# Fewer head tiles among the index scores, eight bisection rounds at once, masks behind the values' tiles

## The chip, the core and the metric

The kernel runs on one core of a Trainium2 chip. The time is that of one execution on the device, in microseconds. Three executions of the kernel before took 1706.53, 1705.96 and 1699.86 us; the median is 1705.96. The core's engines are named as the profile names them: PE multiplies matrices (PEld loads its weights), DVE, ACT and POOL work element by element, SP issues most of the DMAs.

## What is computed

One step of a streaming encoder layer on 1024 prompt rows and 64 sample rows of width 1024, all in float32. The normalised input is projected to the heads' queries, keys and values of two attention branches, to index queries, index keys and index weights, and to gates. Branch a attends only to the 256 keys with the best index score of each query (a quarter of the keys for the sample rows); branch b to a band of chunks with a bias. Both are projected, gated, summed and projected again, and an MLP follows. The part that the change touches:

```python
s = relu(einsum('bqhd,bsd->bqhs', q_idx, k_idx))       # 8 index heads of 64
score = einsum('bqh,bqhs->bqs', w_idx, s)              # one score per query and key
score = where(key_chunk <= query_chunk, score, -inf)
_, idx = top_k(score, 256)                             # per query
logits = einsum('bqhd,bqkhd->bhqk', q, k[idx]) * HEAD_DIM ** -0.5
p = softmax(logits);  out = einsum('bhqk,bqkhd->bqhd', p, v[idx])
```

The outputs include the new keys and values of both branches.

## The kernel before

Each float32 factor is split into a high and a low part (`split`), and a product is three matmuls, on lines 156, 157 and 158 (`three`), or two where one factor's parts are stacked (`two`, lines 164 and 165). The input stays in SBUF transposed (`xnT`). Rows are handled in nine tiles: eight of 128 prompt rows and one of 64 sample rows.

*Keys, queries, scores.* `stage_keys(i)` projects index keys and weights of row tile i (264 columns a matmul), `stage_queries(i)` the index queries (320 columns), both into the two `acc` banks of PSUM. Readers of a keys bank are among others `kd` (L311), `aw` (L319) and `sg` (L320). `norms(i)` makes the norm factors, and `stage_scores(i)` turns the keys into columns (`index_keys`, the transposes of L232) and, for row tiles 2 to 7 and the sample tile, multiplies the turned queries with all keys seen so far: for each of eight heads one or two `s` banks of up to 512 columns (four banks in rotation), which ACT rectifies and scales (L381) and DVE adds to the row tile's scores `work` (L383 for the first head, L385 for the others). Row tiles 0 and 1 need no selection, they see at most 256 keys.

*Head tiles.* `project_heads` is a generator: for vb, kb, qb, ka, va and qa in this order it loads and splits 512 columns of weights and multiplies each of the nine row tiles by them, 24 matmuls of 512 columns for a full row tile, then evacuates the result (values by L527; keys and queries by a square L530, a sum L531, a norm factor, L535), turns it (L485) and parts it into high and low (ACT L124, DVE L148 or L491). Each `next` makes one such head tile. The instructions of these last operations are kept in order in the list `parted`, which holds one entry for every tile turned or, of the values, only for branch a. A head tile's accumulator comes from the iterator `turn`: the first `FIRST` tiles use the `acc` banks, later ones by turns `acc` and `wide`, `wide`. While the scores run, the other four banks are the `s` banks; behind the scores these become four `wide` banks. `stage_scores(i, between)` calls `next` behind the heads that the dictionary names, and what is left runs behind the scores (`for _ in heads`).

*Selection.* `choose` finds the 256th best score of each row by bisection on the bits of a float: counts of positive scores (L617), signs (L627 to L636), then 31 rounds. In a round `cand` sets one more bit (L640), DVE counts three row tiles (L617) and ACT three (L622) against it, and L647 and L648 keep the bit or not. `mask_out(j)` then makes the mask of one of the six row tiles on DVE (L666 to L673, the scan of L669 among them) and POOL (L674).

*Gates.* `gate` projects 128 gate columns on all rows, in chunks of 384, 384 and 320, and L686 scales the result by row. Behind the fourth gate attention begins.

*What sets the order.* The order on each engine is made when the program is built: a scheduler places each recorded instruction as its inputs and buffers allow, and `tc.issue_after(x)` keeps instructions from being placed ahead of instruction x. Round `30 - b` is bound in this way to `parted[(30 - b) * 38 // 31]`, so that the rounds spread over the head tiles, and the masks to the last weight split of the gates.

Of the kernel before, what the change touches and what calls it, by code (L numbers as in the profile page):

```python
# [24 lines left out]
NT = TP // P  # L25
# [5 lines left out]
DFF = 4096  # L31
EPS = 1e-6
RING = 5
FIRST = 8
WARM = 18
BIG = 1e30
HIDDEN = -2.0e38
# [7 lines left out]
def kernel(  # L45
# [80 lines left out]
    last = {}  # L126
# [212 lines left out]
    def stage_queries(i):  # L339
        if i < 2:  # L340
            return
        rows = P if i < NT else TS
        qd = state[i][-3]
        z0, _ = project(i, acc(), parts["queries"], SPLIT)
        copy(qd[:rows, 0:5, 0, :], z0[:rows, :320].rearrange("p (h d) -> p h d", d=HD))
        apply_rope(qd[:rows, :, 0, :], i, rows, H)
        nc.gpsimd.tensor_copy(qd[:rows, :, 1, :], qd[:rows, :, 0, :])
# [84 lines left out]
    def norms(i):  # L432
        stage_norms(i)
        if i + 2 <= NT:
            xts[i + 2] = load_x(i + 2)
# [4 lines left out]
    cut_piece(2, x2)  # L440
    stage_keys(4)
    stage_keys(5)
    with tc.issue_after(last["projected"].ins):
        norms(2)
        norms(3)
        x4 = take_piece(4)
        for nm, g in (("qa", qnorm_a), ("ka", knorm_a), ("kb", knorm_b)):
            load(gains[nm], bcast(g, HD))
        for half in (slice(0, HD), slice(HD, P)):
            load(gain_qb[half], bass.AP(tensor=qnorm_b.tensor, offset=qnorm_b.offset, ap=[[1, HD], [1, 1]]))  # L450
        nc.gpsimd.tensor_scalar(gain_qb, gain_qb, HD ** -0.5, 1.0, op0=ALU.mult, op1=ALU.mult)
        for i in range(3):
            stage_scores(i)
    stage_queries(4)
    stage_queries(5)
    cut_piece(3, x3)
    with tc.issue_after(last["projected"].ins):
        norms(4)
# [102 lines left out]


    heads = project_heads()
    stage_scores(NT - 3, {7: heads})
    stage_scores(NT - 2, {3: heads, 7: heads})
    stage_scores(NT - 1, {3: heads, 7: heads})
    stage_scores(NT, {3: heads, 7: heads})
    close_pool("ix")

    masks = open_pool("masks")  # L570
# [34 lines left out]
    def choose(vector, scalar):  # L605
# [30 lines left out]
            nc.vector.tensor_scalar(w, w, col(sgn, j), None, op0=ALU.mult)  # L636
        nc.vector.memset(bits, 0)
        for b in range(30, -1, -1):
            with tc.issue_after(parted[(30 - b) * 38 // 31]):
                nc.vector.tensor_scalar(cand, bits, 1 << b, None, op0=ALU.bitwise_or)  # L640
            for j, w in enumerate(ws):
                against = col(cand.bitcast(F32), j)
                if j < nv:
                    count(j, w, against, ALU.is_lt)
                else:
                    balance(j, w, against)
            nc.vector.tensor_tensor(ok, cnt, lim, op=ALU.is_le)  # L647
            nc.vector.copy_predicated(bits, ok, cand)  # L648
# [67 lines left out]
    with tc.issue_after(state["last"].ins):  # L716
        for _ in range(TOPK_S // 8):
            m8 = tk.tile([TS, 8], F32, tag="m8", name="m8", bufs=2)
            nc.vector.max(out=m8, in_=work_s)
            nc.vector.match_replace(out=work_s, in_to_replace=m8, in_values=work_s, imm_value=TAKEN)  # L720
        nc.vector.tensor_scalar(mask_s, work_s, 0.5 * (HIDDEN + TAKEN), -BIG, op0=ALU.is_gt, op1=ALU.mult)
        mask_out = choose([2, 3, 4], [5, 6, 7])
    nc.sync.dma_start(mask_below[TS:], mask_s)
    todo = [(mix, h) for mix in "ba" for h in range(H)]
    first_head = load_head(*todo[0], kv)
# [8 lines left out]
    for g in range(0, EARLY, 4):  # L734
        ws = []
        for k in range(KB):
# [3 lines left out]
            lo = pj.tile([P, 512], F32R, tag="wlo", name="wlo", bufs=11)  # L740
            split(raw, hi, lo, lo_on_vector=True)
            ws.append((hi, lo))
        lows = last["lo"]
        for q in range(4):
            gate(g + q, [(h[:, q * P:(q + 1) * P], l[:, q * P:(q + 1) * P]) for h, l in ws])
            while behind and q == 2:
# [2 lines left out]
            if g + q == EARLY - 2:  # L749

                with tc.issue_after(last["turned"].ins):
                    nc.scalar.activation(warm, eps, AF.Exp)

        with tc.issue_after(lows.ins):
            for j in range(6):
                mask_out(j)
    for nm in ("tk", "pj", "works", "fw"):
        close_pool(nm)

# [728 lines left out]
```

## Time and profile before

| | |
|---|---|
| median of three executions | 1705.96 us |
| the profiled execution, its own time | 1701.1 us |
| its span, first to last instruction | 1699.3 us |
| mean granted clock of PE | 0.996 |
| PE, DVE, ACT, POOL busy | 1678.4, 1169.3, 934.4, 393.1 us |
| head tiles behind the scores begin | 163.06 us |
| first bisection round, first mask, attention | 186.4, 411.6, 460.8 us |

The profile is of one execution, and all its times are microseconds from the span's start. Matmuls are pipelined in it: the time of one matmul is longer than the distance to the next one's start, and it is that distance which counts for PE. A bracket behind a row, such as `[2.39 <-POOL kd L333]`, is the idle time of the engine ahead of that instruction, and the instruction that ended it.

### The profile page before, as it was taken

Reading aid. Unit: us, or ns where it says so; the run is one execution under the profiler, and the core shown is the slowest. Engines: PE = TensorE matmul, PEld = TensorE weight load, DVE = VectorE, ACT = ScalarE, POOL = GpSimd, SP = SyncE. Lnnn points to the kernel's source line nnn. Section 1 sums busy time; section 2 is a strip of 40 time slices with the busy share of each in tenths; the row PEclk is TensorE's granted clock in tenths of the full one; section 3 lists DMA queues with packets and bytes.
Section 4 is the critical chain, followed back from the end, with each engine's and each line's share of the span. In section 5 each row is a group of like instructions: output and inputs, shape, how many; then the busy total and the mean of one; then the engine's idle time right before and its main releaser. Section 6 shows DMA issues by size and latency. Waiting matters only on the chain.

```text
span 1699.3 us, 30465 instructions
## 1 busy us (share of the span) xinstructions
PE 1678.4 (99%) x10501; PEld 1543.6 (91%) x10501; DVE 1169.3 (69%) x2748; ACT 934.4 (55%) x1876; POOL 393.1 (23%) x524
## 2 busy tenths in 40 slices
PE   9999999999889999999999999999999999999999
PEld 8987888889889999999999999999999988888887
DVE  7855898879757788874454347666687649656794
ACT  8765688784256777774443347544454346343431
POOL 4434313506243343432343440000000000000000
PEclk9999999999989999999999999999999999999999
DMA  8135366663388877645544459555566599765652
GB/s 277 37 118 155 112 170 169 185 218 94 109 196 194 205 177 174 162 113 162 167 146 145 174 168 311 172 186 182 178 209 196 196 293 300 231 205 174 199 188 90
DMA packets 281195, 303.11 MB, mean 178 GB/s; under 512 B 40209, under 2 KB 202513, under 8 KB 281041
## 3 DMA queue, kind: packets, MB, share of 16 engines
q1 hardware_dynamic: 251920, 265.63, 54.0%
q10 hardware_dynamic: 29120, 35.53, 6.0%
q8 instruction: 83, 1.36, 0.3%
q14 instruction: 72, 0.58, 0.1%
HBM read 207.98 MB, written 93.08 MB: 177 GB/s over the span
## 4 chain that ended last, share of the span: by engine, by line
PE 70%; DMA 5%; DVE 3%; ACT 2%; issue 1%; POOL 1%; SPq 0%; ACTq 0%; DVEq 0%
PE x L156 6%; PE x L157 6%; PE x L158 6%; PE acc L156 6%; PE acc L158 6%; PE acc L157 6%; PE pt L814 3%; PE pg L156 2%; PE pe L156 2%; PE pg L158 2%; PE pe L158 2%; PE pe L157 2%; PE pg L157 2%; PE po L830 2%; PE s L164 2%; PE po L829 2%
## 5 line engine op out<-in xcount | busy, mean ns | idle before, releaser
L124 ACT ACTIVATE hi<-hw 128x1024 fp32r<-128x1024 f32 (+1 forms) x108 | 99.9, 932 | 159.2 <-PE x L158 56.3
L157 PE MATMUL x<-lo,hi 128*128 128x512 f32 (+1 forms) x440 | 169.5, 385 | 0.0
L158 PE MATMUL x<-hi,lo 128*128 128x512 f32 (+1 forms) x440 | 169.1, 385 | 0.0
L156 PE MATMUL x<-hi 128*128 128x512 f32 (+1 forms) x440 | 165.1, 385 | 0.0
L148 DVE TENSOR_TENSOR lo<-hw,hi 128x1024 fp32r<-128x1024 f32 (+1 forms) x108 | 113.8, 1061 | 47.9 <-ACT hi L124 46.5
L150 POOL TENSOR_TENSOR lo<-raw,hi 128x512 fp32r<-128x512 f32 x74 | 98.4, 1339 | 130.1 <-ACT hi L124 115.6
L124 ACT ACTIVATE hi<-raw 128x512 fp32r<-128x512 f32 x104 | 64.3, 626 | 96.3 <-PE acc L157 20.8
L622 ACT ACTIVATE nth<-work,cand 128x768 bf16<-128x768 f32 (+2 forms) x93 | 96.6, 1039 | 13.5 <-DVE cand L640 9.5
L826 DVE TENSOR_TENSOR pl<-pt,ph 128x512 fp32r<-128x512 f32 (+2 forms) x152 | 90.9, 615 | 16.7 <-ACT ph L124 16.3
L157 PEld LDWEIGHTS x<-lo,hi 128*128 128x128 f32 x440 | 82.7, 188 | 16.6
L156 PEld LDWEIGHTS x<-hi 128*128 128x128 f32 x440 | 82.7, 188 | 16.6
L158 PEld LDWEIGHTS x<-hi,lo 128*128 128x128 f32 x440 | 82.7, 188 | 16.5
L156 PE MATMUL acc<-xnT,hi 128*128 128x384 f32 (+1 forms) x288 | 97.2, 337 | 0.0
L157 PE MATMUL acc<-xnT,hi 128*128 128x384 f32 (+1 forms) x288 | 95.1, 330 | 0.0
L158 PE MATMUL acc<-xnT,lo 128*128 128x384 f32 (+1 forms) x288 | 94.9, 330 | 0.0
L157 PE MATMUL wide<-wlo,xnT 128*128 128x512 f32 x240 | 94.2, 394 | 0.0
L158 PE MATMUL wide<-whi,xnT 128*128 128x512 f32 x240 | 93.7, 391 | 0.0
L156 PE MATMUL wide<-whi,xnT 128*128 128x512 f32 x240 | 92.2, 394 | 1.3 <-DVE work_s L385 1.3
L124 ACT ACTIVATE ph<-pt 128x512 fp32r<-128x512 f32 (+3 forms) x168 | 80.1, 514 | 23.3 <-PE pt L814 18.6
L801 POOL TENSOR_SCALAR mw<-mw,sm 128x640 f32<-128x640 f32 (+1 forms) x64 | 56.7, 885 | 127.6 <-DVE sm L800 123.4
L164 PE MATMUL s<-kh,qT 128*128 128x384 f32 (+4 forms) x208 | 77.1, 372 | 3.5 <-DMA kh<-kT_b 1.9
L830 PE MATMUL po<-pl,vhl 128*128 128x256 f32 (+1 forms) x304 | 79.5, 293 | 0.4 <-DVE pl L826 0.3
(693 smaller groups left out, 5731.9 us busy)
## 6 DMA issues: line engine op xcount, KB each, us to landing
hw<-h SPq DMA_DIRECT2D x108, 256.0 KB, 3.1
hw<-in_w_down_dram SPq DMA_DIRECT2D x108, 256.0 KB, 3.7
wraw<-in_w_in_dram SPq DMA_DIRECT2D x56, 256.0 KB, 2.8
h<-h ACTq DMA_DIRECT2D x32, 272.0 KB, 2.2
raw<-in_w_out_dram SPq DMA_DIRECT2D x32, 256.0 KB, 3.0
raw<-in_w_up_dram SPq DMA_DIRECT2D x32, 256.0 KB, 3.4
out_dram<-t SPq DMA_DIRECT2D x24, 256.0 KB, 2.8
g_dram<-gate SPq DMA_DIRECT2D x32, 192.0 KB, 2.4
```

What stands on the lines that cost most here:

```text
L124: return nc.scalar.activation(out, in_, AF.Copy)
L148: last["lo"] = nc.vector.tensor_sub(lo, raw, hi)
L150: nc.gpsimd.tensor_sub(lo, raw, hi)
L156: nc.tensor.matmul(out, sh, mh, start=(opens and i == 0), stop=False, skip_group_check=resumes)
L157: nc.tensor.matmul(out, sh, ml, start=False, stop=False, skip_group_check=resumes)
L158: last = nc.tensor.matmul(out, sl, mh, start=False, stop=(closes and i == n - 1), skip_group_check=resumes)
L164: first = nc.tensor.matmul(out, s, mh, start=(i == 0), stop=False)
L622: nc.scalar.activation(sign[:, :w.shape[1]], w, AF.Sign, bias=against, scale=-1.0, accum_out=col(cnt, j))
L801: nc.gpsimd.tensor_scalar(m[:rows, :n], m[:rows, :n], sm[:rows, 6:7], 1.0, op0=ALU.mult, op1=ALU.mult)
L814: nc.tensor.transpose(ps[:krows, oo:oo + qrows], m[:qrows, kc:kc + krows], ident[:qrows, :qrows])
L826: nc.vector.tensor_sub(pl[:kr, a:b], ps[:kr, a:b], ph[:kr, a:b])
L830: nc.tensor.matmul(dst, vhl[:krows, vt, :], pl[:krows, oo:oo + width], start=False, stop=(idx == n - 1))
```

## The change

1. Index keys and queries. `stage_queries(4)` and `stage_queries(5)` are recorded right behind `stage_keys(5)`, and the block that holds the norms 2 and 3 and the first three `stage_scores` follows behind them; the norms 2 and 3 are taken out of the block. The block waits for the last projection recorded, which now is that of query tile 5.
2. Head tiles. `FIRST` is 5 and not 8, and `next(heads)` is called four times in the scores and not seven.
3. Rounds. The first eight rounds (b from 30 to 23) are bound to nothing; the other 23 to `parted[(22 - b) * 28 // 23]`.
4. Masks. The six masks are bound to `parted` 30, 32, 33, 35, 36 and 38, which are value tiles of branch a, and no longer to the gates' weights.

```diff
-FIRST = 8
+FIRST = 5
...
     stage_keys(4)
     stage_keys(5)
+    norms(2)
+    norms(3)
+    stage_queries(4)
+    stage_queries(5)
     with tc.issue_after(last["projected"].ins):
-        norms(2)
-        norms(3)
...
         for i in range(3):
             stage_scores(i)
-    stage_queries(4)
-    stage_queries(5)
...
-    stage_scores(NT - 3, {7: heads})
-    stage_scores(NT - 2, {3: heads, 7: heads})
+    stage_scores(NT - 3)
+    stage_scores(NT - 2, {7: heads})
     stage_scores(NT - 1, {3: heads, 7: heads})
-    stage_scores(NT, {3: heads, 7: heads})
+    stage_scores(NT, {7: heads})
...
-            with tc.issue_after(parted[(30 - b) * 38 // 31]):
+            with tc.issue_after(parted[(22 - b) * 28 // 23]) if b < 23 else ExitStack():
                 nc.vector.tensor_scalar(cand, bits, 1 << b, None, op0=ALU.bitwise_or)
...
         mask_out = choose([2, 3, 4], [5, 6, 7])
+        for j, at in enumerate((30, 32, 33, 35, 36, 38)):
+            with tc.issue_after(parted[at]):
+                mask_out(j)
...
-        lows = last["lo"]
...
-        with tc.issue_after(lows.ins):
-            for j in range(6):
-                mask_out(j)
```

What this makes of the order is seen at three places. The first is PE behind the matmuls of key tile 5 (`wkh`, `wkl` are the parts of the key weights, `wqh`, `wql` those of the query weights, `kd` the keys to be turned). A row with a minus is in the kernel before only, with a plus in the changed one only:

```order
 L157 MATMUL acc<-wkl_154,xnT 128x264
 L158 MATMUL acc<-wkh_153,xnT 128x264
-L232 MATMUL pt<-ident,kd 128x128 x2
 L156 MATMUL acc<-wqh_265,xnT 128x320
 L157 MATMUL acc<-wql_266,xnT 128x320
```

and 48 matmuls further on:

```order
 L157 MATMUL acc<-wql_275,xnT 128x320
 L158 MATMUL acc<-wqh_274,xnT 128x320
+L232 MATMUL pt<-ident,kd 128x128 x2
 L156 MATMUL acc<-wkh_144,xnT 128x264
 L157 MATMUL acc<-wkl_145,xnT 128x264
```

The two transposes have moved behind the matmuls of query tiles 4 and 5.

The second place is PE at the end of the scores. Before, the score matmuls (`s`, of 512 columns for row tile 7 and of 192 for the sample rows) stand between the matmuls of head tiles:

```order
L156 MATMUL acc_2318<-whi_2186,xnT_105 128x512
L164 MATMUL s_1898<-kih_134,qiT_1782 128x512
L165 MATMUL s_1898<-kil_135,qiT_1782 128x512
L157 MATMUL acc_2318<-wlo_2187,xnT_105 128x512
L158 MATMUL acc_2318<-whi_2186,xnT_105 128x512
L156 MATMUL acc_2318<-whi_2192,xnT_105 128x512
L164 MATMUL s_1903<-kih_134,qiT_1782 128x512
L165 MATMUL s_1903<-kil_135,qiT_1782 128x512
L164 MATMUL s_1967<-kih_134,qiT_1952 64x192
L165 MATMUL s_1967<-kil_135,qiT_1952 64x192
```

In the changed kernel:

```order
L164 MATMUL s_1760<-kih_134,qiT_1720 128x512
L165 MATMUL s_1760<-kil_135,qiT_1720 128x512
L164 MATMUL s_1765<-kih_134,qiT_1720 128x512
L165 MATMUL s_1765<-kil_135,qiT_1720 128x512
L164 MATMUL s_1770<-kih_134,qiT_1720 128x512
L165 MATMUL s_1770<-kil_135,qiT_1720 128x512
```

All 32 matmuls of row tile 7 and the 16 of the sample rows stand in one run, and the first `wide` head tile follows.

The third place is DVE at the gates. Before:

```order
L686 TENSOR_TENSOR gate<-wide,spread 128x384
L686 TENSOR_TENSOR gate<-acc,spread 128x320
L667 TENSOR_SCALAR need<-cnt 128x1
L669 SCALAR_TENSOR_TENSOR nth<-ones,seen 128x896
L671 SCALAR_TENSOR_TENSOR seen<-nth,need,seen 128x896
L686 TENSOR_TENSOR gate<-wide,spread 128x384 x2
L673 TENSOR_TENSOR seen<-seen 128x896
L666 TENSOR_SCALAR seen,cnt<-work_119,thr 128x1024
```

In the changed kernel the gates have DVE to themselves, and the masks stand between the value tiles' last operations (L148):

```order
L673 TENSOR_TENSOR seen<-seen 128x384
L666 TENSOR_SCALAR seen,cnt<-work_115,thr 128x512
L148 TENSOR_TENSOR pair<-t,pair 128x8x64
L668 TENSOR_SCALAR seen<-work_115,thr 128x512
L667 TENSOR_SCALAR need<-cnt 128x1
L669 SCALAR_TENSOR_TENSOR nth<-ones,seen 128x512
```

The mask of the last row tile stands among the first tiles of qa.

## The prediction

> **What bounds the kernel now.** I read the page first, then the waits of PE up to the start of attention, then the windows by stage, then the timeline at the places that the change touches. The page (busy us, share of the span, instructions; below it the chain):
>
> ```profile
> PE 1678.4 (99%) x10501; PEld 1543.6 (91%) x10501; DVE 1169.3 (69%) x2748; ACT 934.4 (55%) x1876; POOL 393.1 (23%) x524
> PE 70%; DMA 5%; DVE 3%; ACT 2%; issue 1%; POOL 1%; SPq 0%; ACTq 0%; DVEq 0%
> ```
>
> PE is busy for all but 21 us of 1699.3. The change removes no matmul, so it can only move PE's idle time. Every engine has the same order in both kernels from the start of attention, at about 460 us, so what it can win is what PE waits for before that. The waits of PE from 0 to 460 us (line waited <- releaser: us in total, times, longest):
>
> ```profile
> PE pt L731 <- DVE pair L491: 2.7, 2, 1.4
> PE pt L232 <- POOL kd L333: 2.4, 1, 2.4
> PE wide L156 <- DVE work_s L385: 1.3, 1, 1.3
> PE s L300 <- DVE zeros L297: 1.1, 1, 1.1
> PE wide L156 <- DVE gate L686: 0.5, 1, 0.5
> PE pt L485 <- POOL t L214: 0.5, 1, 0.5
> ```
>
> Four shorter ones make 1.1 us more. Without the wait at the program's first matmul (L300, untouched) that is 8.5 us, or 0.5% of the time, and 0.5% (8.5 us) is about what a measurement of this kernel can tell from no change. **No gain that could be told from nothing is to be had here, while a loss has no such ceiling.** The windows (start:end, length, then busy us of PE, PEld, DVE, ACT, POOL, with PE's granted clock behind them) say which engine has room:
>
> ```profile
> 120.00:140.00 20.00, 20.00 (x90) 15.63 (x89) 9.33 (x14) 10.85 (x19) 3.83 (x4) 1.00 0.25 98
> 160.00:180.00 20.00, 18.66 (x85) 15.26 (x85) 18.58 (x73) 4.04 (x10) 3.99 (x9) 1.00 0.29 81
> 200.00:220.00 20.00, 20.00 (x95) 16.56 (x94) 18.73 (x46) 15.94 (x33) 12.05 (x11) 1.00 0.71 207
> 430.00:440.00 10.00, 7.72 (x47) 7.15 (x48) 9.95 (x17) 1.31 (x3) 1.96 (x3) 1.00 0.42 127
> 470.00:480.00 10.00, 6.61 (x27) 6.08 (x28) 2.33 (x11) 2.84 (x9) 1.62 (x3) 0.55 1.16 229
> ```
>
> Among the scores (120 to 140) PE is full while DVE and ACT are half idle: the head tiles between the scores cover what DVE needs. In the bisection (200 to 220) DVE and ACT are both near full and PE is still covered. At the gates (430 to 440) DVE is full and PE idles.
>
> **Part one, keys behind queries 4 and 5.** Here is where the 2.4 us wait stands, PE and then DVE:
>
> ```profile
> 32.35 0.27 PE L232 MATMUL pt<-ident,kd 128*128 128x128 f32 x1
> 35.01 0.33 PE L232 MATMUL pt<-ident,kd 128*128 128x128 f32 x1 [2.39 <-POOL kd L333]
> 35.62 0.39 PE L156 MATMUL acc<-wqh,xnT 128*128 128x320 f32 x1 [0.28 <-DVE by_row L284]
> 35.33 0.15 DVE L320 TENSOR_SCALAR sg<-acc 128x8 f32<-128x8 f32 x1
> ```
>
> The change puts query 4's matmuls where the transposes stood. There are two accumulator banks, keys 4 and 5 hold both, and the last reader of keys 4's bank is the DVE operation of L320, which runs at 35.33 and ends at 35.48. It stands at the same place of DVE's order in both kernels. The first query matmul therefore cannot start before about 35.5; it started at 35.62. The wait is handed from one instruction to the next, and the two transposes are still paid for later. I take 0; bounds -0.4 (start at 35.5, and a transpose hidden) to +0.5 (a new wait of the size of the `by_row` one behind the moved key transposes).
>
> **Part two, four head tiles instead of seven.** `next(heads)` is called seven times before and four times after; what was recorded among the scores as tiles on the `acc` banks is 256 matmuls before and 178 after, so 78 matmuls move behind the scores. They cost the same there. What they leave behind is the last stretch of the scores, 32 matmuls of 512 columns for tile 7 and 16 of 192 for the sample rows, with no head tile between them. Each pair fills one of four score banks, which ACT rectifies (L381) and DVE folds in (L385); the first `wide` tile behind it reuses a score bank and waits for the last L385, as it does now. The rows for the costs:
>
> ```profile
> 154.89 0.75 DVE L385 SCALAR_TENSOR_TENSOR work<-s,sg,work 128x512 f32<-128x512 f32 x1 [1.45 <-ACT s L381]
> 155.55 0.40 DVE L383 TENSOR_SCALAR work_s<-s,sg 64x192 f32<-64x192 f32 x1
> 156.06 0.41 DVE L385 SCALAR_TENSOR_TENSOR work_s<-s,sg,work_s 64x192 f32<-64x192 f32 x1
> 145.59 1.24 ACT L381 ACTIVATE s<-s,aw 128x512 f32<-128x512 f32 x2
> 161.38 0.25 PE L164 MATMUL s<-kih,qiT 128*64 128x192 f32 x1
> 161.47 0.25 PE L165 MATMUL s<-kil,qiT 128*64 128x192 f32 x1
> 163.06 0.50 PE L156 MATMUL wide<-whi,xnT 128*128 128x512 f32 x1 [1.34 <-DVE work_s L385]
> 163.63 0.39 PE L158 MATMUL wide<-whi,xnT 128*128 128x512 f32 x1
> 163.86 0.40 PE L156 MATMUL wide<-whi,xnT 128*128 128x512 f32 x1
> ```
>
> Start to start, DVE takes 155.55 - 154.89 = 0.66 us for a 512 wide score and 156.06 - 155.55 = 0.51 for a 192 wide one. ACT needs about 0.6 (1.24 for two), so DVE sets the pace. The tail is 16 x 0.66 + 8 x 0.51 = 14.6 us on DVE, plus about 1.4 until its first operand is there (a pair of matmuls and one ACT operation of 0.66), 16.0 in all. PE's own work there is 32 x 0.23 + 16 x 0.09 = 8.8 us (0.23 from 163.63 to 163.86, 0.09 from 161.38 to 161.47). PE idles 16.0 - 8.8 = 7.2 us, where it idles 1.3 now: **+5.9 us**. Lower bound +3: DVE keeps to ACT's 0.58 a wide score and the first 1.4 are hidden behind the last head tile's matmuls (9.3 + 4.1 - 8.8 - 1.3). Upper bound +9: DVE comes to the tail some 3 us late with what the head tiles left it.
>
> The first eight bisection rounds are not tied to a head tile any more. Before, the first round stands behind a kb tile's L491, at 186. It has to wait for the counts and signs (L617, L636), about 11 us behind the scores, so it moves up to some 10 us behind the end of the scores. Until then ACT is idle in both kernels (4.04 us busy of 20). The cost of a round on ACT, and of what a kb tile needs there:
>
> ```profile
> 185.63 0.59 ACT L530 ACTIVATE t<-wide 128x512 f32<-128x512 f32 x1
> 187.51 0.58 ACT L124 ACTIVATE pair<-pt 128x512 fp32r<-128x512 f32 x1
> 188.46 0.30 ACT L132 ACTIVATE sd<-ss,by_row 128x8 f32<-128x8 f32 x1
> 192.50 0.94 ACT L622 ACTIVATE nth<-work,cand 128x768 bf16<-128x768 f32 x1
> 193.56 1.04 ACT L622 ACTIVATE nth<-work,cand 128x896 bf16<-128x896 f32 x1
> 194.80 1.13 ACT L622 ACTIVATE nth<-work,cand 128x1024 bf16<-128x1024 f32 x1
> ```
>
> A round is 0.94 + 1.04 + 1.13 and three short accumulator reads, about 3.5; a tile 0.59 + 0.58 + 0.30 = 1.5; together 5.0, and up to 0.9 more while the next `cand` comes round through DVE. PE needs 24 x 0.23 = 5.5 us for a tile and some 0.4 for its four transposes. PE has 159 matmuls (36 us) queued between the end of the scores and the first kb transpose. Counting the chain to that transpose through ACT's order (two value tiles, three rounds, then L530, the norm's chain on DVE and ACT, L535 behind the fifth `cand`, POOL) I arrive at 35 us. It is even: I take **+1**, between 0 and +8 (the first rival). Rounds 9 to 31 keep the pace of now, 23 over 27 tiles against 31 over 37, and cost nothing.
>
> **Part three, masks behind the value tiles.** At the gates:
>
> ```profile
> 430.36 0.65 PE L731 MATMUL pt<-ident,by_row 128*128 128x128 f32 x4 [1.31 <-DVE pair L491]
> 434.30 0.85 PE L731 MATMUL pt<-ident,by_row 128*128 128x128 f32 x5 [1.38 <-DVE pair L491]
> 435.69 0.44 PE L156 MATMUL wide<-xnT,whi 128*128 128x384 f32 x1 [0.55 <-DVE gate L686]
> ```
>
> DVE is full there with the masks, of which the scan is the largest group:
>
> ```profile
> L669 DVE TENSOR_TENSOR_SCAN nth<-ones,seen 128x384 f32<-128x384 f32 (+5 forms) x6 | 9.8, 1640 | 0.0
> ```
>
> With L666, L668, L671 and L673 they are about 29 us. Moved among the va tiles they take the slots that the rounds leave, which are now finished some ten tiles sooner: six masks over eight tiles are 3.6 us of DVE a tile of 5.9, where a round with its final counts stood before. PE should lose nothing there (bound +2). The waits of 1.31, 1.38 and 0.55 go: **-3.2 us**, bounds -3.8 (the 0.53 of L485 with them) and -1.0 (the transposes then wait for the 5.9 us tile cadence instead). It does not start attention's loads any sooner than PE reaches the last gate, since these are issued when PE has finished it; so a shorter gate stage is worth its own length only.
>
> **The sum:** 0 + 5.9 + 1 - 3.2 = +3.7 on the profiled execution's 1701.1, thus 1704.8. That execution lies 3.0 below the mean of the three runs (1704.1) and 4.9 below their median; with 3.0 added I come to **1708 us**, and its own range is 1702 to 1713.
>
> **Rivals.** *First, slower: the eight rounds at once starve PE of banks.* Place: ACT, 10 to 45 us behind the scores. It decides if ACT needs over 5.9 us for a round and a tile. With two weight splits a tile (0.58 each, as L124 above) the 5.0 becomes 6.1, with the `cand` latency 7.0: 1.1 over, times eight tiles, +9 in place of +1, so 1716. For it: DVE and ACT at 18.7 and 15.9 of 20 already. Against: those 15.9 hold the splits and 0.84 rounds a tile already (31 over 37), and 0.16 rounds more (0.6 us in 5.9) leave ACT at 90%.
>
> *Second: PE's clock falls in the half idle tail.* PE would be busy 8.8 of 16.0 there. A busy share of 6.61 in 10 went with a granted clock of 0.55 at 470 to 480, one of 7.72 with 1.00 at 430 to 440. Rows of both sides of the drop:
>
> ```profile
> 474.15 0.41 PE L830 MATMUL po<-pl,vhl 128*128 128x256 f32 x1
> 474.36 0.41 PE L829 MATMUL po<-ph,vhl 128*128 128x256 f32 x1
> 481.71 0.28 PE L830 MATMUL po<-pl,vhl 128*128 128x256 f32 x1
> 481.83 0.28 PE L829 MATMUL po<-ph,vhl 128*128 128x256 f32 x1
> ```
>
> The same matmul takes 0.21 and 0.12 start to start, 1.75 times. A 512 pair then takes 0.81 instead of 0.46 and PE, not DVE, sets the tail: 16 x 0.81 + 8 x 0.32 = 15.5, 0.9 more than DVE's 14.6. Behind the tail some 3 us (from 477.93, where PE resumes, to 481) run slow, 1.4 lost. +2.3, so 1710. Against: the idle pieces of the tail are under 0.5 us each; at 470 to 473 they were 1.9 and 1.1. The Trainium skill has this rule: in "TensorE: Matmul & The Clock Gate", section "A second HAM failure mode: psum-queue depth-cycling", a PE that idles a little between groups of matmuls, because it cycles through PSUM banks, lets the clock gate oscillate. By it the tail would throttle; the row at 430 to 440, with idle pieces of 1.3 us and a clock of 1.00, speaks against it.
>
> *Third, a gain: the tail is shorter than counted.* If DVE enters it with nothing queued and ACT's results come in pairs, +3 instead of +5.9, no stall in the rounds and -3.8 at the gates make -0.8, and with the key wait truly gone -3: 1701 to 1703. Against: the L320 row above.
>
> *Fourth, nothing moves,* because waits only change place everywhere, the masks' among them: 1704.
>
> **How the numbers follow.** Forecast 0.50, first rival 0.20, second 0.10, third 0.14, fourth 0.06. Low end: the third case (1701) less the 4 us by which single executions lie below others, 1697. High end: the first (1716) plus 3, 1719. Faster by over 0.5% needs the third case and luck, 0.06; slower by over 0.5% (above 1714.5) is the first case, a part of the second and a tail of the forecast, 0.25; the rest, 0.69, lies within.
>
> **What would show it.** In the new profile: PE's wait `pt <- POOL kd` gone and one of about the same size at the first `acc` of the queries, at 35.5; a row of short PE waits on L385 and one of a few us at the first `wide`, 6 to 8 us together, with DVE back to back; the first L622 some 10 us behind that point, and waits of PE at L485 below 2 us; no wait at L731 and the gates' DVE windows well below 9.9. I am wrong if PE's waits before 460 us sum to less than today's 8.5, or if the rounds hold PE for over 5 us.

## The result and the profile after

The changed kernel is slower: 1720.47 us (median of six, 1714.33 to 1722.08) against 1703.26 us of the kernel before on the same chip. The ratio is 1.0094, with a 95% interval from 1.0071 to 1.0118, or 16 us. The forecast was 1708 us and no difference that can be told, the range 1697 to 1719: the time lies outside. The profiled executions, one of each kernel, took 1721.5 and 1701.1 us.

The busy times of the changed kernel, and the waits of its PE up to 460 us (line waited <- releaser: total, times, longest):

```profile
PE 1689.4 (98%) x10501; PEld 1545.7 (90%) x10501; DVE 1173.5 (68%) x2748; ACT 935.7 (54%) x1876; POOL 389.5 (23%) x524
```

```profile
PE pt L485 <- DVE pair L491: 3.9, 2, 3.1
PE acc L156 <- DVE by_row L284: 3.2, 1, 3.2
PE pt L485 <- POOL t L214: 2.7, 2, 1.8
PE wide L156 <- DVE work_s L385: 1.7, 1, 1.7
PE wide L157 <- POOL wlo L150: 1.4, 2, 0.7
...
PE s L164 <- DVE work L385: 1.1, 4, 0.3
```

The work is the same, the waits are others: L731 is gone, L485 has come. Where the time is lost shows best on PE's own matmuls, since every kernel here has the same 1152 of them for the prompt rows of the head tiles. Before, the first one of qb, the first one of ka, the last one of qa, and the first matmul of attention:

```profile
201.37 0.39 PE L156 MATMUL wide<-whi,xnT 128*128 128x512 f32 x1
253.88 0.39 PE L156 MATMUL wide<-whi,xnT 128*128 128x512 f32 x1
400.07 0.39 PE L158 MATMUL wide<-whi,xnT 128*128 128x512 f32 x1
460.06 0.22 PE L164 MATMUL s<-kh,qT 128*128 128x128 f32 x1
```

The same four in the changed kernel:

```profile
210.54 0.39 PE L156 MATMUL wide<-whi,xnT 128*128 128x512 f32 x1
271.01 0.39 PE L156 MATMUL wide<-whi,xnT 128*128 128x512 f32 x1
423.87 0.39 PE L158 MATMUL wide<-whi,xnT 128*128 128x512 f32 x1
479.94 0.33 PE L164 MATMUL s<-kh,qT 128*128 128x128 f32 x1 [0.58 <-DVE gate L686]
```

PE is 9.2 us late at the first qb matmul, 17.1 at the first of ka, 23.8 at the last of qa, and 19.9 at attention; the spans differ by 20.4, so what lies behind the start of attention is nearly even. In words: up to the first qb matmul, with the tail of the scores and the first rounds, 9 are lost; 8 more while the qb tiles are multiplied; 7 between ka and the end of qa, where the masks are; and the gates give 4 back. One execution can be 2 or 3 us late or early by its first 80 us alone, as will be seen, so these are sizes and not exact prices. The windows of the changed kernel around the first two places (length, then busy us of PE, PEld, DVE, ACT, POOL, and PE's granted clock):

```profile
150.00:155.00 5.00, 3.73 (x9) 2.96 (x10) 4.57 (x18) 0.03 (x1) 1.03 (x6) 0.55 0.19 59
155.00:160.00 5.00, 5.00 (x19) 4.03 (x18) 5.00 (x19) 0.10 (x1) 0.00 (x0) 0.77 0.01 2
...
230.00:235.00 5.00, 3.06 (x14) 2.19 (x12) 4.96 (x6) 2.66 (x5) 3.30 (x3) 1.00 0.75 201
235.00:240.00 5.00, 3.79 (x12) 3.03 (x13) 4.06 (x13) 4.90 (x11) 0.00 (x0) 0.58 0.60 164
240.00:245.00 5.00, 5.00 (x20) 4.10 (x19) 4.58 (x17) 5.00 (x11) 0.00 (x0) 0.74 0.48 119
```

Behind each stall the clock is down to 0.55 to 0.77 for some 5 us, which PE pays on top of it.

### The profile page after: what moved, and what is told of

Its sections match the earlier page's. It is cut to its first block, busy times and chain, and to the rows that moved or that the text cites. A ratio compares the mean times of both kernels' runs of the same rounds, so it can differ in the third digit from the quotient of the medians.

```text
span 1719.7 us, 30488 instructions
## 1 busy us (share of the span) xinstructions
PE 1689.4 (98%) x10501; PEld 1545.7 (90%) x10501; DVE 1173.5 (68%) x2748; ACT 935.7 (54%) x1876; POOL 389.5 (23%) x524
## 4 chain that ended last, share of the span: by engine, by line
PE 71%; DMA 4%; DVE 3%; issue 1%; ACT 1%; SPq 1%; POOL 0%; ACTq 0%; DVEq 0%; POOLq 0%
PE acc L156 7%; PE acc L158 7%; PE acc L157 7%; PE x L156 6%; PE x L157 6%; PE x L158 6%; PE pt L812 3%; PE po L828 2%; PE pe L156 2%; PE pg L156 2%; PE pg L158 2%; PE pe L158 2%; PE s L164 2%; PE pg L157 2%; PE pe L157 2%; PE po L827 2%
## 5 line engine op out<-in xcount | busy, mean ns | idle before, releaser
L148 DVE TENSOR_TENSOR lo<-hw,hi 128x1024 fp32r<-128x1024 f32 (+1 forms) x108 | 114.4, 1066 | 48.0 <-ACT hi L124 46.7
L150 POOL TENSOR_TENSOR lo<-raw,hi 128x512 fp32r<-128x512 f32 x74 | 98.3, 1337 | 130.7 <-ACT hi L124 125.8
L124 ACT ACTIVATE hi<-raw 128x512 fp32r<-128x512 f32 x104 | 64.3, 626 | 95.6 <-PE acc L157 20.6
L157 PE MATMUL wide<-wlo,xnT 128*128 128x512 f32 x256 | 103.0, 404 | 1.6 <-POOL wlo L150 1.4
L156 PE MATMUL wide<-whi,xnT 128*128 128x512 f32 x256 | 100.6, 403 | 2.4 <-DVE work_s L385 1.7
L824 DVE TENSOR_TENSOR pl<-pt,ph 128x512 fp32r<-128x512 f32 (+2 forms) x152 | 90.9, 615 | 16.3 <-ACT ph L124 15.7
L158 PE MATMUL wide<-whi,xnT 128*128 128x512 f32 x256 | 101.5, 398 | 0.0
L799 POOL TENSOR_SCALAR mw<-mw,sm 128x640 f32<-128x640 f32 (+1 forms) x64 | 56.4, 882 | 127.4 <-DVE sm L798 123.2
```

The lines of the kernel that those rows point to most:

```text
L124: return nc.scalar.activation(out, in_, AF.Copy)
L148: last["lo"] = nc.vector.tensor_sub(lo, raw, hi)
L150: nc.gpsimd.tensor_sub(lo, raw, hi)
L156: nc.tensor.matmul(out, sh, mh, start=(opens and i == 0), stop=False, skip_group_check=resumes)
L157: nc.tensor.matmul(out, sh, ml, start=False, stop=False, skip_group_check=resumes)
L158: last = nc.tensor.matmul(out, sl, mh, start=False, stop=(closes and i == n - 1), skip_group_check=resumes)
```

## The experiments

Unless something else is said, a difference is against the kernel before, measured on the same chip, and 0.1% is 1.7 us.

### Keys behind queries 4 and 5, alone

```diff
     stage_keys(5)
+    norms(2)
+    norms(3)
+    stage_queries(4)
+    stage_queries(5)
     with tc.issue_after(last["projected"].ins):
-        norms(2)
-        norms(3)
...
-    stage_queries(4)
-    stage_queries(5)
```

> The kernel before with query tiles 4 and 5 ahead of the turned keys alone. The wait of 2.4 us at L232 becomes one of about 3 us at the first query matmul: within 1 us of before, ratio 0.9995 to 1.0010. The rival, that the wait is won elsewhere: 2 us faster.

Ratio 1.0012 (1.0002 to 1.0022): no gain, and a loss of at most a few us. Its PE in the timeline:

```profile
36.09 0.39 PE L156 MATMUL acc<-wqh,xnT 128*128 128x320 f32 x1 [3.55 <-DVE by_row L284]
```

The wait is handed on. It is somewhat longer than the two waits of before, as the two transposes stand behind it now. The run is not quite the part alone: the scheduler also ordered DVE otherwise at the gates, with two of the qa prompt tiles' L491 behind the first mask and not three. In its trace PE is 5.4 us late at the first qb matmul (206.81) and then takes 56.4 us from the last qa matmul to attention, where the kernel before takes 60.0. So the +2 may be a loss of a few us ahead and a gain at the gates.

### Head tiles, alone

```diff
-FIRST = 8
+FIRST = 5
...
-    stage_scores(NT - 3, {7: heads})
-    stage_scores(NT - 2, {3: heads, 7: heads})
+    stage_scores(NT - 3)
+    stage_scores(NT - 2, {7: heads})
     stage_scores(NT - 1, {3: heads, 7: heads})
-    stage_scores(NT, {3: heads, 7: heads})
+    stage_scores(NT, {7: heads})
```

> The kernel before with the head tiles' part of the change alone (FIRST 5, four calls of next in the scores). Theory A, from the two traces: the tail of the scores costs by itself what it costs in the changed kernel, about 4 us of idle PE and 2.6 us in which PE's clock is down behind it: +7 us on before, ratio 1.004, with granted clock near 0.55 in the 5 us behind the tail. Rival B: the tail costs what it does only together with the rounds; alone 0 to +2.

Ratio 1.0036 (1.0026 to 1.0047), +6 us. The tail costs by itself. PE reaches the first `wide` tile at 151.10, where 78 matmuls fewer are done than at 163.06 before; 78 x 0.227 = 17.7, so it is 5.8 us late. About 2 of these are not the tail's. Up to the first head tile PE has the same order in both kernels, and heads_only already starts that tile 1.85 us later (77.55 against 75.70). Its clock was lower in one early window, here of the kernel before and then of heads_only:

```profile
35.00:40.00 5.00, 4.71 (x32) 4.54 (x33) 4.97 (x36) 4.61 (x20) 2.11 (x9) 1.00 0.74 236
35.00:40.00 5.00, 4.33 (x18) 4.17 (x19) 4.97 (x36) 4.47 (x19) 2.65 (x10) 0.66 0.65 211
```

Behind the tail the clock is down too (window of heads_only), and at the first qb matmul (209.53) PE is 8.2 us late:

```profile
150.00:155.00 5.00, 3.90 (x9) 3.12 (x10) 4.57 (x18) 0.05 (x1) 1.03 (x6) 0.50 0.19 59
```

### The tail filled

heads_only with extra matmuls into the score banks of the tail, which the scores then overwrite:

```diff
                 ps = bank("s")
+                for _ in range(0 if i < NT - 1 else 1 if i < NT else 2):
+                    nc.tensor.matmul(ps[:rows, :min(w, 320)], qiT[:, h, :rows],
+                                     kih[:, k0 + c:k0 + c + min(w, 320)], start=True, stop=True)
                 two(ps[:rows, :w], ...)
```

> heads_only with extra matmuls into the same score bank ahead of each score of the tail (one of 320 columns ahead of a 512 wide score, two of 192 ahead of a sample score; they are overwritten), so that PE is busy for most of the tail while DVE still sets its pace. If the clock is part of the tail's cost (A), the clock stays at 1.00 behind the tail and the kernel is 2 to 3 us faster than heads_only. If the cost is DVE's pace alone (B), the two are equal.

Ratio 1.0036 (1.0022 to 1.0051), the same as heads_only. A `wide` tile and the window behind the tail in heads_filled:

```profile
153.44 0.50 PE L156 MATMUL wide<-whi,xnT 128*128 128x512 f32 x1 [1.48 <-DVE work_s L388]
```

```profile
150.00:155.00 5.00, 3.52 (x25) 2.68 (x23) 4.15 (x15) 1.88 (x5) 1.03 (x6) 1.00 0.04 12
```

The clock stays at 1.00, so the fall goes with the idle tail. But the first `wide` comes 2.3 us later (153.44 against 151.10): the fill costs about what it saves. That the slow clock is a part of the tail's 6 us is shown by the rows; that it can be saved is not.

### Eight rounds at once, alone

```diff
-            with tc.issue_after(parted[(30 - b) * 38 // 31]):
+            with tc.issue_after(parted[(22 - b) * 38 // 23]) if b < 23 else ExitStack():
```

> The kernel before with eight rounds at once alone (the other 23 spread over the same 37 tiles as before). A, from the traces: the rounds put DVE's and ACT's work for a tile behind rounds, PE waits at L485 for L491, and the clock falls once more: +5 to +9 us, waits at L485 of 2 us and more within 80 us behind the scores. B: the rounds hurt only because the moved head tiles shift them: 0 to +2.

Ratio 1.0054 (1.0041 to 1.0068), +9 us. By its trace 6 us are lost from the first qb to the last qa matmul (204.7 us, 198.7 before). Another 4 stand at the gates, where this kernel still makes its masks (64.3 us from there to attention, 60.0 before). Two windows of it:

```profile
440.00:445.00 5.00, 2.02 (x13) 1.51 (x11) 4.76 (x8) 0.60 (x1) 0.83 (x2) 0.91 0.38 107
445.00:450.00 5.00, 3.24 (x11) 2.72 (x10) 4.93 (x9) 0.71 (x2) 0.83 (x1) 0.50 0.41 131
```

In the kernel before the clock stayed at 1.00 at this place; here the waits are a little longer and it falls.

### The rounds spread evenly over fewer tiles

In the changed kernel, and then on the kernel before:

```diff
-            with tc.issue_after(parted[(22 - b) * 28 // 23]) if b < 23 else ExitStack():
+            with tc.issue_after(parted[(30 - b) * 28 // 31]):
```

> The changed kernel, but all 31 rounds spread evenly over the first 28 tiles (none at once; the last is bound to the same tile). If the eight rounds at once are the cause of the waits at L485 and the fallen clock 60 to 95 us behind the scores (theory A), this is 4 to 8 us faster than the changed kernel, ratio to before about 1.005, and has no wait of 3 us at L485. If any 31 rounds in 28 tiles are too dense (rival B), it is within 2 us of the changed kernel, and the waits come elsewhere in the bisection.

Ratio 1.0153 (1.0137 to 1.0169): 10 us slower than the changed kernel, which neither theory held. (The last round is bound to tile 27 here and to 26 in the changed kernel, so the two do not end at quite the same tile.) The trace shows both a gain and a larger loss. From the first qb to the first ka matmul PE takes 54.9 us, where the changed kernel takes 60.5 and the kernel before 52.5: the eight rounds at once do cost some 5 us there. But the last round begins at 374 us and not at 350, the last mask at 422 and not at 398, and from the first va matmul to attention PE takes 170.6 us in place of 157.9.

```diff
-            with tc.issue_after(parted[(30 - b) * 38 // 31]):
+            with tc.issue_after(parted[(30 - b) * 34 // 31]):
```

> The kernel before with its 31 rounds bound to tiles 0 to 32 (34 in place of 38 in the rule); masks at the gates as before. Theory A: the pace of rounds per head tile decides, because a round (3.5 us on ACT, in which DVE's next bit and all behind it wait) and a tile's own ACT work must fit in a tile's 5.9 us: waits at L485 in the ka and va tiles, +4 to +8 us on before. Rival B: masks_spread was slow through its masks alone: 0 to +2 here.

Ratio 1.0058 (1.0045 to 1.0071), +10 us for 31 rounds over 33 tiles in place of 37, with nothing else edited. By its trace only 3 us of it are lost among the head tiles (201.9 us from the first qb to the last qa matmul, 198.7 before). The gates lose 5 (64.8 us from there to attention, 60.0 before), where PE waits 3.0 us for L491 and 2.3 for a gate's L686. So a denser pace costs little by itself; most of this run's loss is the order that it leaves at the gates.

### DVE's part or ACT's part of the rounds

In the changed kernel the three counts of one engine are left out in each round (the rows concerned never take a bit, so the masks of their row tiles select other keys):

```diff
         nc.vector.memset(bits, 0)
+        for j in (3, 4, 5):
+            nc.vector.memset(col(lim, j), -1e9)
...
             for j, w in enumerate(ws):
+                if j in (3, 4, 5):
+                    continue
```

(0, 1 and 2 for DVE's part.)

> The changed kernel without DVE's three counts in each of the 31 rounds (2.2 us a round; the masks of row tiles 2, 3 and 4 are then wrong, everything else runs as it is). Theory A: DVE's load behind the scores makes PE wait at L485. Then the waits of 150 to 380 us go, and the kernel is 6 to 10 us faster than the changed one (ratio to before about 1.004). Rival B: ACT's load does: 0 to 2 us faster, since a round then still takes ACT's 3.5 us.

> The changed kernel without ACT's three counts in each round (3.5 us a round; the masks of row tiles 5, 6 and 7 are then wrong). If DVE's load makes PE wait (A), 0 to 4 us faster than the changed kernel; if ACT's does (B), 6 to 10 us faster.

Without ACT's counts the ratio is 1.0040 (1.0027 to 1.0054), 9 us faster than the changed kernel. Without DVE's it is 1.0154 (1.0135 to 1.0172), 10 us slower than it. A window of 20 us in the bisection, of the changed kernel, then of light_act, then of light_dve:

```profile
220.00:240.00 20.00, 15.99 (x68) 12.27 (x67) 18.80 (x46) 14.77 (x29) 9.19 (x8) 0.90 0.67 190
```

```profile
220.00:240.00 20.00, 19.65 (x94) 15.46 (x93) 18.24 (x61) 8.11 (x17) 9.10 (x8) 1.00 0.76 210
```

```profile
220.00:240.00 20.00, 18.04 (x84) 13.66 (x83) 14.19 (x34) 16.28 (x34) 11.35 (x9) 1.00 0.76 214
```

With DVE at 18.2 of 20 and ACT light, PE is nearly full; with DVE at 14.2 and ACT as it was, PE loses 2 us in 20. From the first qb to the first ka matmul PE takes 60.5 us in the changed kernel, 61.6 without DVE's counts and 53.5 without ACT's, where the kernel before takes 52.5. So it is ACT's part of the rounds that costs there, and a full DVE alone does not stop PE. DVE waits for ACT's counts for 16.3 us of the 197 from 160 to 357 in the changed kernel, and for 37.3 of 200 when its own counts are gone.

How late a tile gets is seen in the distance from PE's transposes (L485) to DVE's L491 behind them. The first and the seventh kb tile of the kernel before:

```profile
184.50 0.60 PE L485 MATMUL pt<-ident,t 128*128 128x128 f32 x4
185.77 0.69 DVE L491 TENSOR_TENSOR pair<-pt,pair 128x512 fp32r<-128x512 f32 x1 [3.92 <-ACT pair L124]
216.58 0.60 PE L485 MATMUL pt<-ident,t 128*128 128x128 f32 x4
219.69 0.69 DVE L491 TENSOR_TENSOR pair<-pt,pair 128x512 fp32r<-128x512 f32 x1
```

The same in the changed kernel, where the seventh L491 is the one at 235.37 in the fence below:

```profile
190.70 0.60 PE L485 MATMUL pt<-ident,t 128*128 128x128 f32 x4
195.92 0.69 DVE L491 TENSOR_TENSOR pair<-pt,pair 128x512 fp32r<-128x512 f32 x1 [0.68 <-ACT pair L124]
223.73 0.60 PE L485 MATMUL pt<-ident,t 128*128 128x128 f32 x4
```

The distance is 1.3 and 3.1 us before, 5.2 and 11.6 in the changed kernel, and 4.8 and 6.4 without ACT's counts. So the chain behind PE starts late with the early rounds, and falls back further until PE has to wait. Here is the longest wait of the changed kernel, in PE, DVE and ACT:

```profile
236.21 0.66 PE L485 MATMUL pt<-ident,t 64*128 64x64 f32 x4 [3.14 <-DVE pair L491]
229.68 3.65 DVE L640 TENSOR_SCALAR cand<-bits 128x6 int32<-128x6 int32 x1
233.37 0.61 DVE L617 TENSOR_SCALAR_CACHE_REDUCE seen<-work,cand 128x384 bf16<-128x384 f32 x1
235.37 0.69 DVE L491 TENSOR_TENSOR pair<-pt,pair 128x512 fp32r<-128x512 f32 x1
230.54 0.58 ACT L124 ACTIVATE pair<-pt 128x512 fp32r<-128x512 f32 x1
233.43 0.93 ACT L622 ACTIVATE nth<-work,cand 128x768 bf16<-128x768 f32 x1 [2.31 <-DVE cand L640]
```

L491 had its operand at 231.1 and could have run. It stands in DVE's order behind a round's `cand` and three counts. Of its 4.3 us, 2.2 are the end of that `cand`, which takes 3.65 us here, and 2.0 the counts. DVE does not wait for ACT at this place; ACT itself waits 2.31 us for `cand`. The transposes of the next tile need the bank that L491 reads.

light_dve's other loss stands at the masks: POOL's weight split takes five times its 1.3 us beside DVE's scan and the operations behind it, and PE waits 4.8 us for it. POOL, then DVE, of light_dve (its scan is on line 673, since four lines were added above it):

```profile
386.79 6.40 POOL L150 TENSOR_TENSOR wlo<-wraw,whi 128x512 fp32r<-128x512 f32 x1 [2.91 <-ACT whi L124]
386.66 2.01 DVE L673 TENSOR_TENSOR_SCAN nth<-ones,seen 128x896 f32<-128x896 f32 x1
```

### The small operations beside POOL

The 3.65 us of L640 above are spent beside POOL operations that follow each other from 229.51 to 233.30. The changed kernel with `bits` and `cand` stored 8 bytes apart:

```diff
-        bits, cand, ok = (small(x, I32) for x in ("bits", "cand", "ok"))
+        wider = lambda nm: tk.tile([P, nb, 2], I32, name=nm)
+        ok = small("ok", I32)
+        bits, cand = (wider(x)[:, :, 0] for x in ("bits", "cand"))
```

> The changed kernel with the bits and cand columns stored 8 bytes apart, so that the few-element DVE operations on them (L640, L648) run on strided data. In the trace L640 takes 0.16 us when POOL is idle and up to 3.65 us beside POOL, and the 3.65 stands right ahead of the longest wait of PE. If contiguous 32 bit data is what makes this operation queue behind POOL, L640 stays below 0.3 us beside POOL and the kernel is 2 to 6 us faster than the changed one. If the operation queues behind POOL whatever its layout, nothing changes: within 2 us.

Ratio 1.0097 (1.0082 to 1.0113), as the changed kernel; by the two intervals a gain of 2 or 3 us is not excluded. `cand` (line 642 in this kernel) still takes up to 1.24 us beside POOL, so the layout is not the whole reason. In the profiled execution the 3.1 us wait at L485 did not come back, and from the first qb to the first ka matmul PE takes 55.0 us and not 60.5; yet the median over all executions did not move. How much the one long `cand` costs in most executions stays open.

### Head tiles as before, the rest of the change kept

```diff
-FIRST = 5
+FIRST = 8
...
+    stage_scores(NT - 3, {7: heads})
+    stage_scores(NT - 2, {3: heads, 7: heads})
     stage_scores(NT - 1, {3: heads, 7: heads})
+    stage_scores(NT, {3: heads, 7: heads})
```

> The changed kernel with the head tiles as before (FIRST 8, seven calls). heads_only cost 6 us on before. If the parts add up, this is 5 to 8 us faster than the changed kernel, ratio about 1.005 to 1.006, with the clock at 1.00 behind the scores. If the rounds take up any slack that the tail leaves (the parts overlap), 0 to 3 us faster.

Ratio 1.0111 (1.0097 to 1.0125): no faster than the changed kernel. The 6 us of the tail are saved and lost again; PE's longest waits at L485 are now

```profile
PE pt L485 <- POOL t L214: 6.5, 3, 5.5
PE pt L485 <- DVE pair L491: 1.8, 2, 1.5
```

The longest, of 5.5 us, stands at the first qa tiles (416.93 us). With 78 matmuls fewer behind the scores the rounds and masks have less of PE's work to stand beside; that this is why the 6 us are lost again is argued and not shown. The parts do not add up.

### The masks

The changed kernel with the masks back at the gates:

```diff
-        for j, at in enumerate((30, 32, 33, 35, 36, 38)):
-            with tc.issue_after(parted[at]):
-                mask_out(j)
...
+        lows = last["lo"]
...
+        with tc.issue_after(lows.ins):
+            for j in range(6):
+                mask_out(j)
```

> The changed kernel with the masks put back to the gates. As predicted before the run (masks at the value tiles cost nothing, the gates win 3.2): 3 us slower than the changed kernel, ratio to before about 1.011. From the traces (masks among the value tiles cost 5 to 6 us of PE and win 3 at the gates): 2 to 3 us faster than the changed kernel, ratio about 1.008.

Ratio 1.0070 (1.0057 to 1.0084), 4 us faster than the changed kernel by the middle values; the two intervals still overlap. And with the masks among the values but without the rule for equal scores (L667 to L673 left out):

> The changed kernel whose masks leave out the rule for equal scores (L667 to L673: 19 of the masks' 29 us on DVE; of equal scores at the threshold none is then taken). If the masks' time on DVE is what PE waits for between 380 and 420 us, the waits at L485 and at the wlo splits there go and it is 3 to 5 us faster than the changed kernel. If their place is harmless, as the prediction held, it is within 1 us.

Ratio 1.0072 (1.0050 to 1.0094), also 4 us faster, with overlapping intervals again. The traces agree with both: from the first va to the last qa matmul PE takes 101.8 us in the changed kernel, 98.3 in un_masks and 98.0 in no_ties. The kernel before takes 95.1, so some 3 of the 7 us that are lost there are not the masks'. Two windows of the changed kernel, then of no_ties:

```profile
380.00:400.00 20.00, 18.91 (x80) 14.38 (x79) 19.96 (x33) 7.10 (x13) 6.12 (x5) 1.00 0.60 175
400.00:420.00 20.00, 18.11 (x86) 14.48 (x85) 13.34 (x35) 3.94 (x9) 10.52 (x17) 1.00 0.19 53
```

```profile
380.00:400.00 20.00, 20.00 (x92) 16.58 (x91) 11.59 (x27) 5.35 (x11) 10.66 (x17) 1.00 0.35 116
400.00:420.00 20.00, 20.00 (x99) 16.59 (x97) 11.81 (x33) 6.23 (x13) 8.09 (x15) 1.00 0.42 114
```

The masks among the value tiles keep the first qa tile's norm chain and POOL's weight splits waiting; without most of their DVE time PE is full.

Wider spacing does not help. The kernel before with rounds over tiles 0 to 32 and one mask behind every second tile from 34 to 44:

> The kernel before with its rounds bound to tiles 0 to 32 (34 in place of 38 in the rule) and the masks one behind every second tile from 34 to 44, in values and qa, none at the gates. If the gates' 3 us can be won when DVE has room for a mask (as the prediction held), 2 to 4 us faster than before, ratio 0.998. If the masks cost PE among the head tiles whatever their spacing, 0 to 4 us slower.

Ratio 1.0105 (1.0091 to 1.0119), +18 us. rounds_denser, with the same rounds and the masks at the gates, is at +10. The longest waits are for qa's norm chain and the gates' first bank, behind masks (`wide` <- `rs` L142 5.0 us, `wide` <- `t` L535 3.5 us).

Taking one operation of the masks (L668) to POOL at the gates of the kernel before, in place of DVE:

```diff
-            nc.vector.tensor_scalar(same[:, :n], w, col(thr, j), None, op0=ALU.is_equal)
+            nc.gpsimd.tensor_scalar(same[:, :n], w, col(thr, j), 1.0, op0=ALU.is_equal, op1=ALU.mult)
```

> The kernel before with one of the masks' operations (L668, 5 us in all) on POOL, which is idle at most of the gates. If DVE's load at the gates is what PE waits for there (3.2 us at L731 and L686), 1 to 2.5 us faster than before, ratio 0.999. If POOL beside DVE takes longer for both, or DVE waits for POOL's result, 0 to 4 us slower.

Ratio 1.0002 (0.9993 to 1.0012): nothing.

### Where at the gates the masks begin

un_masks holds a surprise. Its masks are at the gates, DVE is as full as before, and PE does not wait (window of un_masks; the kernel before has 7.72 of 10 at its place):

```profile
430.00:440.00 10.00, 10.00 (x66) 9.70 (x66) 9.55 (x24) 3.48 (x8) 3.82 (x5) 1.00 0.44 126
```

Its PE takes 55.3 us from the last qa matmul to attention, where the kernel before takes 60.0. In its order of DVE the first mask stands behind all but one of the qa prompt tiles' L491; in the kernel before three of them stand among the first four masks. So the kernel before was tried with nothing changed but the instruction to which the masks are bound, the L491 of the last qa prompt tile (masks_late), or the one ahead of it (masks_late2, `parted[-3]`):

```diff
-        lows = last["lo"]
...
-        with tc.issue_after(lows.ins):
+        with tc.issue_after(parted[-2]):
             for j in range(6):
                 mask_out(j)
```

> The kernel before with the six masks bound to the last but one turned tile (the L491 of the last qa prompt tile) and not to the gates' weights; head tiles, rounds and keys as before. In un_masks, where the masks stand at the gates but behind the qa tiles, PE was busy 10.0 of 10 us there although DVE was full, so the waits of the kernel before come from qa's L491 standing behind masks. If so, the waits at L731 and L686 (3.2 us) go: 2 to 4 us faster than before, ratio 0.998. If masks at the gates cost PE wherever they stand, or the last mask ends behind the last gate and holds attention up, 0 to 4 us slower.

> The same, bound one tile sooner (the L491 ahead of that one), so that the masks end about 5 us sooner. If masks_late suffers from masks that end too late, this is the faster of the two; if one qa L491 behind masks is enough to stop PE, the slower. By the first theory 2 to 4 us faster than before, ratio 0.998.

masks_late: 1695.54 us, ratio 0.9967 (0.9957 to 0.9977). masks_late2: ratio 0.9979 (0.9970 to 0.9989). They are faster than the kernel before by 6 and 4 us. Two windows at the gates of masks_late:

```profile
430.00:440.00 10.00, 10.00 (x61) 9.74 (x60) 9.93 (x20) 0.38 (x2) 1.21 (x2) 1.00 0.34 120
440.00:450.00 10.00, 10.00 (x64) 9.74 (x63) 9.89 (x16) 1.87 (x3) 0.97 (x2) 1.00 0.28 76
```

DVE makes the same masks in less time, 32 us from the first (425.83) to the last where the kernel before took 40, and PE does not wait once between 400 us and the start of attention at 457.41. The gates' 3.2 us were not a matter of DVE's load, but of what stood ahead of L491. From the last qa matmul to attention PE takes 55.4 us in place of 60.0, a gain of 4.6, which lies inside the interval of the ratio (4 to 7 us). masks_late2, with one prompt tile's L491 behind the first mask's start, has no wait there either and begins attention at 457.37; where it loses 2 us to masks_late is not shown.

## Why the prediction was wrong, by its own steps

*What bounds the kernel.* This held: the best of the runs, masks_late, wins 6 of the 8.5 us, and the loss, which had no such ceiling, is 16.

*Part one, the keys.* The mechanism was right: the wait was passed to the first query matmul, at 35.84 us. The size, 0 with bounds -0.4 to +0.5, may be too small. keys_only measures +2 with an interval from 0.3 to 3.7, and its trace shows more lost ahead and something won at the gates.

*Part two, the tail.* The count of DVE's slots was right for the tail itself: from the last head tile matmul ahead of it (135.02) to the first `wide` (151.27) are 16.2 us in the changed kernel, and 16.0 were counted. That heads_only measures +6 where +5.9 was forecast is partly luck. The scheduler left half of row tile 7's scores among the head tiles there, its tail is 10.9 us long (140.19 to 151.10), and without the 2 us that were lost at 35 us PE is some 4 late at its end. The rest is the second rival, which had 0.10: a clock of 0.50 behind the tail. The row at 430 to 440 us, which was held against it, did not decide. The rule of the Trainium skill cited there ("TensorE: Matmul & The Clock Gate", section "A second HAM failure mode: psum-queue depth-cycling") agrees with heads_only at 0.50 and heads_filled at 1.00, though one fall is seen here and no oscillation.

*Part two, the rounds: the step that failed first.* "It is even: I take +1." This term is the one that is wrong by most. PE loses 8 us between the first qb and the first ka matmul, which ACT's counts cause, since light_act loses 1 there; rounds_only measures +9 in all, 4 of it at the gates. That "the rounds hold PE for over 5 us" was among the prediction's own signs of being wrong. The count went only as far as the first kb transpose, and PE does not wait there. It left out how far L491 is behind by then, 5.2 us in place of 1.3, and that this would grow to 11.6 at the seventh tile (PE's first wait at L485 is at 212 us, the longest at 236).

The first rival (0.20, priced at +9) came near in size and named the right engine. Its place was wrong, not 10 to 45 but 60 to 85 us behind the scores, and so was its way at the longest wait: PE waits there for L491 behind a long `cand` and three counts in DVE's queue, and not because ACT evacuates late. Why the lag grows is open. The pace is not denser than before (one round every 6.5 us from 192 to 237 us, one every 6.1 from 186 to 235 in the kernel before), and the one long `cand` beside POOL has a part that the runs do not settle. That rounds 9 to 31 would cost nothing held from the first ka to the first va matmul, where both kernels take 51.1 us; while va is multiplied another 2 us are lost.

*Part three, the masks: the second step that failed.* "PE should lose nothing there (bound +2)." un_masks and no_ties put it at 4 us, and so do the traces. The step compared a sum of DVE's time with a sum of room, 3.6 us a tile in 5.9. What decides is what stands behind a mask in DVE's order, here qa's norm chain, and POOL's splits beside it; from its first to its last operation a mask takes up to 9 us there.

*The gates.* -3.2 was right in size: 3.9 by PE's times from the last qa matmul to attention (56.1 us, 60.0 before). The reason given, DVE full with masks, was not: un_masks and masks_late have the masks there and no wait.

*The sum.* In place of 5.9 + 1 - 3.2, the parts measured alone give 6 + 9 + 4 - 3.2, about 16, which is what was measured. That is partly luck: 4 of rounds_only's 9 stand at the gates, where the changed kernel loses nothing, and un_heads gains nothing.

## What to carry to other kernels

A wait for an engine that is 95% busy is not yet a wait for its load: look at what stands ahead of the awaited instruction in its order, and first try to move that. Here, letting the masks begin behind three more of qa's L491, some 14 us later, won what moving the masks away could not. And when work is moved ahead of a chain that feeds another engine, the first link of the chain proves nothing. Look how late the chain is there compared with before, and whether it can catch up, since a loop across two engines delays everything that is queued behind it on both. A part that is tested alone also gets its own order from the scheduler, so its trace has to be read for what else moved.

## What the runs showed of the hardware

PE's clock falls after short, repeated stalls as well as after one long one, and stays down some 5 us: 0.50 behind the tail of heads_only, where no single wait was longer than 1.5 us (with the tail filled, 1.00), and 0.58 in the window with the 3.1 us wait of the changed kernel. A wait does not lower it each time. In the window from 35 to 40 us it is 1.00 in the changed kernel, behind a wait of 3.19 us, 0.69 in keys_only behind one of 3.55, and 0.66 in heads_only behind one of 2.57.

DVE and POOL hold each other up. POOL's split of 512 columns takes 1.3 us and took 6.40 beside DVE's scan and what followed it; DVE's L640 on six columns takes 0.16 us and took 3.65, until the last of a row of POOL operations was over, while L491 and L617, which ran beside POOL in the same stage, kept their 0.69 and 0.61. The Trainium skill has a rule for this in "SBUF — State Buffer", section "SBUF: two separate sides": one pair of ports is shared by the two engines and is locked for a whole instruction, so that the loser waits in full. The 6.40 and the 3.65 agree with such a wait, but both are longer than any one operation of the other engine there (2.01 us on DVE, 1.3 on POOL), so by that rule the loser was passed over more than once. By the strided run, which still shows 1.24 for the same operation, storing the operands apart is no full way around it.
